# A two-block transformer kernel: the gate table's reads go to GpSimd's queue, and the second token block's search is paced more slowly

## The chip, the cores and the metric

One core of a Trainium2 chip runs the whole program. The metric is device time in microseconds (us), lower is better. A time shown as a median comes from runs without a profile; the trace is of one further, profiled execution.

## What is computed

A sequence of 256 tokens (plus 16 meta tokens), 1024 channels, float32, goes through two blocks. The first block mixes with a state-space scan and then applies PEER, a layer of 16,384 single-neuron experts:

```
q = (t @ w_q).reshape(T, 8, 2, 128)
s = einsum('thsd,hskd->thsk', q, sub_keys)
v_half, i_half = top_k(s, 16)
cand = v_half[:, :, 0, :, None] + v_half[:, :, 1, None, :]
best, pos = top_k(cand, 16)                      # per token and head
experts = i1 * 128 + i2 ;  gates = softmax(best)
act = gelu(einsum('td,tkd->tk', xb, expert_u[experts])) * gates
out = einsum('tk,tkd->td', act, expert_v[experts])
```

The second block is a gated linear recurrence, a convolutional feed-forward layer, windowed attention with sinks and a second feed-forward layer. The change touches only the work around PEER.

## The kernel before

**Dense experts.** The kernel does not gather experts. It multiplies all 256 tokens with all 16,384 rows of `expert_u` (the first expert stage, 128 weight chunks of 128 experts each), applies GELU, multiplies by a gate that is zero where an expert was not chosen, and multiplies the result with all of `expert_v` (the second expert stage, again 128 chunks). The products `hact` stay in on-chip memory between the two stages.

**Weights.** Every weight chunk is a 512 KB tile `raw`, loaded by SyncE (SP) in one queue, in order, into four buffers. ScalarE rounds it to a high part `wh` (three buffers), VectorE subtracts to get a low part `wl` (three buffers), and TensorE makes three products of high and low parts for each chunk. The load of a chunk waits until `wl` of the chunk four before it has been made, since that frees its buffer.

**The gates** of the two blocks of 128 tokens come in two ways. For the first block (`tb` 0), the search (`topk1(0)`, `topk2(0)`) finds the places, and GpSimd scatters 128 columns of values into a table `gtab` in device memory (128 indirect writes, zeroed earlier). In the second expert stage `w_split(j2)` reads a piece `gts` of that table for each pair of chunks (64 reads of 128 KB, `g_load`, two buffers) and VectorE multiplies it into `hact`; ScalarE then makes `wth` (the rounded `hact`) and VectorE `wtl` (its low part), which are TensorE's stationary operands. For the second block (`tb` 1), `topk1(1)` and `topk2(1)` search, a TensorE transpose puts the indices into `idxT`, and `g_side(1)` builds one-hot tiles `oA`, `oB`, multiplies them on TensorE into `sm` and multiplies the gates into `hact`, four tokens a step, during the first expert stage.

**What sets the order.** Main-line code calls `wa` for each chunk of the first expert stage. After each chunk `tick()` advances the side generators by their rates: a generator that yields a cost c at rate r consumes c / r chunks. That is the order in which instructions are emitted; a scheduler then places them on each engine from its own estimates, and every engine runs its list strictly in order. `g_load(j2 + 2)` is emitted in `w_split(j2)`, right after the multiplication that empties the buffer; loads 0 and 1 are emitted three pairs before the end of the first expert stage.

Of the kernel before, what the change touches and what calls it, by code (L numbers as in the profile page):

```python
# [208 lines left out]
def build(tc, a, out):  # L209
    nc = tc.nc  # L210
    top = ExitStack()
    with top:
# [54 lines left out]
        V, S, PE, SP = nc.vector, nc.scalar, nc.tensor, nc.sync  # L267
# [157 lines left out]
        def wait(cond):  # L425
            while not cond():
                yield
# [314 lines left out]
        gtv = gtab.rearrange("(a c) o -> a (c o)", a=128)  # L742
# [282 lines left out]
        def score(tb, c):  # L1025
            return scores[:, tb * 16 + c]
# [19 lines left out]
        def top16(vals, idxs, src, w, part):  # L1046
            if part == 0:
                V.max(out=vals[:, 0:8], in_=src)
                V.max_index(out=idxs[:, 0:8], in_max=vals[:, 0:8], in_values=src)
                V.match_replace(out=w, in_to_replace=vals[:, 0:8], in_values=src, imm_value=-3.0e38)  # L1050
            else:
                V.max(out=vals[:, 8:16], in_=w)
                V.max_index(out=idxs[:, 8:16], in_max=vals[:, 8:16], in_values=w)

        def topk1(tb):
            for c in range(16):
                yield from wait(lambda: c in ust["sc"])
                w = gp.tile([128, 128], F, name="sw", bufs=1)
                for part in range(2):
                    top16(vh[:, c], ih[:, c], score(tb, c), w, part)  # L1060
                    yield 0.4 if part else 0.6
            ust["topk"] = tb
# [77 lines left out]
        def after(ins, others):  # L1140
            for other in others:
                tc.add_manual_dep(ins.ins, other.ins.name, mybir.DependencyInfo(
                    mybir.DependencyClass.Sync, mybir.DependencyReason.DATA), reason="the same places")
# [54 lines left out]
        def paced(gen, rate):  # L1198
            for c in gen:
                yield (1.0 if c is None else c) / rate  # L1200

        def peer_side():
            yield from paced(topk1(0), 1.3)
            yield from paced(topk2(0), 1.3)

            yield from paced(topk1(1), 1.1)
            yield from paced(topk2(1), 1.1)
            yield from paced(g_side(1), 1.25)

        skp = Pool(0, 16, 8)  # L1210
# [17 lines left out]

        add_side(u_norm())
        add_side(peer_side())  # L1230
        for c in range(16):
            qs = sk_load(c)
# [29 lines left out]
        gts = {}  # L1262

        def g_load(j2):
            gts[j2] = gtp.tile([128, 2, 128], F, name="gts")
            ins = SP.dma_start(gts[j2].rearrange("p j t -> p (j t)"), gtv[:, j2 * 256:(j2 + 1) * 256])
            after(ins, last)

            tc.add_manual_dep(ins.ins, st["mm"].ins.name, mybir.DependencyInfo(
                mybir.DependencyClass.NoSync, mybir.DependencyReason.SCHED_ONLY), reason="order")  # L1270

        for j2 in range(64):
            if j2 == 61:
                g_load(0)
                g_load(1)
            if j2 == 46:
                while ust["topk"] < 1:
                    step_sides()
            pp = bank("acc").rearrange("p (j t) -> p j t", j=2)
            for j in range(2):  # L1280
                wa(pp[:, j], xTh, xTl, T0, 256)
            u_post(j2, pp)
# [6 lines left out]
        def w_split(j2):  # L1289
            wth = wp.tile([128, 2, 256], FR, name="wth")  # L1290
            wtl = wp.tile([128, 2, 256], FR, name="wtl")
            g = gts.pop(j2)
            for _, tsl, hv_ in Hact(2 * j2, 2 * j2 + 2, 0, 128):
                tt(hv_, hv_, g, OP.mult)
            if j2 + 2 < 64:
                g_load(j2 + 2)
            for _, tsl, hv_ in Hact(2 * j2, 2 * j2 + 2, 0, 256):
                act(wth[:, :, tsl], hv_, AF.Copy)
                tt(wtl[:, :, tsl], hv_, wth[:, :, tsl].bitcast(F), OP.subtract)
            wts[j2] = (wth, wtl)  # L1300
# [473 lines left out]
```

## Time and profile before

| what | value |
|---|---|
| median of 3 runs | 1685.29 us (1683.22 to 1690.29) |
| the profiled execution's own time | 1680.89 us |
| its span in the trace | 1679.1 us |
| TensorE busy | 1657.2 us |
| VectorE busy | 1219.5 us |
| ScalarE busy | 949.6 us |
| GpSimd busy | 242.6 us |

The profiled execution is the reference for every duration below; it is 4.4 us under the median of the other runs. Matmuls overlap, so that TensorE counts as busy even where its rate drops: the rate is read from how many matmuls start in a stretch, or from the distance between starts.

### The profile page before, as it was taken

Reading aid. Unit: us, or ns where it says so; the run is one execution under the profiler, and the core shown is the slowest. Engines: PE = TensorE matmul, PEld = TensorE weight load, DVE = VectorE, ACT = ScalarE, POOL = GpSimd, SP = SyncE. Lnnn points to the kernel's source line nnn. Section 1 sums busy time; section 2 is a strip of 40 time slices with the busy share of each in tenths; the row PEclk is TensorE's granted clock in tenths of the full one; section 3 lists DMA queues with packets and bytes.
Section 4 is the critical chain, followed back from the end, with each engine's and each line's share of the span. In section 5 each row is a group of like instructions: output and inputs, shape, how many; then the busy total and the mean of one; then the engine's idle time right before and its main releaser. Section 6 shows DMA issues by size and latency. Waiting matters only on the chain. (4 is left out here: it accounts for less than half of the span.)

```text
span 1679.1 us, 29135 instructions
## 1 busy us (share of the span) xinstructions
PE 1657.2 (99%) x11114; PEld 1498.8 (89%) x11114; DVE 1219.5 (73%) x2388; ACT 949.6 (57%) x1590; POOL 242.6 (14%) x132
## 2 busy tenths in 40 slices
PE   8999999999999999999999999999999999999998
PEld 6999889999999999877777788998899988899986
DVE  6789768999567874555555666987787757887754
ACT  6877556544478874444444455733565545765543
POOL 0000000187887870000000000000000000000000
PEclk9999999999999999999999999999999999999999
DMA  8844465577766666666666696634566655346663
GB/s 268 284 133 132 151 204 177 164 173 174 206 172 145 149 154 186 196 210 197 205 204 209 221 325 207 188 114 143 164 192 188 187 175 174 101 162 182 187 186 114
DMA packets 118205, 306.59 MB, mean 183 GB/s; under 512 B 28961, under 2 KB 47905, under 8 KB 117810
## 3 DMA queue, kind: packets, MB, share of 16 engines
q1 hardware_dynamic: 99634, 304.67, 58.4%
q0 software_dynamic: 18432, 0.07, 2.7%
q8 instruction: 87, 1.43, 0.4%
q14 instruction: 52, 0.43, 0.1%
HBM read 294.14 MB, written 10.55 MB: 181 GB/s over the span
## 5 line engine op out<-in xcount | busy, mean ns | idle before, releaser
L290 ACT ACTIVATE wh<-raw 128x1024 fp32r<-128x1024 f32 x523 | 552.3, 1057 | 484.4 <-PE acc L272 426.2
L278 DVE TENSOR_TENSOR wl<-raw,wh 128x1024 fp32r<-128x1024 f32 x523 | 634.3, 1222 | 210.6 <-ACT wh L290 206.0
L272 PE MATMUL acc<-xTh,wh 128*128 128x256 f32 (+2 forms) x2184 | 541.0, 286 | 0.3 <-ACT xTh L290 0.3
L272 PE MATMUL acc<-xTl,wh 128*128 128x256 f32 (+2 forms) x2184 | 533.8, 282 | 1.0 <-DVE xTl L278 1.0
L272 PEld LDWEIGHTS acc<-xTh,wh 128*128 128x128 f32 x2184 | 411.4, 189 | 3.3 <-issue 1.7
L272 PEld LDWEIGHTS acc<-xTl,wh 128*128 128x128 f32 x2184 | 412.3, 189 | 2.2 <-DVE xTl L278 1.2
L272 PE MATMUL acc<-xTh,wl 128*128 128x256 f32 (+2 forms) x2184 | 307.0, 282 | 1.8 <-DVE wl L278 1.6
L1150 POOL DMA_INDIRECT gtab<-gval,gplace x128 | 242.4, 1893 | 389.1 <-DVE gplace L287 328.5
L272 PEld LDWEIGHTS acc<-xTh,wl 128*128 128x128 f32 x2184 | 279.1, 188 | 4.0 <-DVE wl L278 3.9
L272 PE MATMUL acc<-wl,wth 128*128 128x512 f32 x512 | 205.7, 402 | 3.0 <-DVE wl L278 2.8
L272 PE MATMUL acc<-wh,wth 128*128 128x512 f32 x512 | 202.2, 395 | 0.0
L272 PE MATMUL acc<-wh,wtl 128*128 128x512 f32 x512 | 161.5, 394 | 0.0
L272 PEld LDWEIGHTS acc<-wl,wth 128*128 128x128 f32 x512 | 96.4, 188 | 37.6 <-DVE wl L278 16.7
L272 PEld LDWEIGHTS acc<-wh,wtl 128*128 128x128 f32 x512 | 96.4, 188 | 22.4
L272 PEld LDWEIGHTS acc<-wh,wth 128*128 128x128 f32 x512 | 96.4, 188 | 20.9 <-ACT wh L290 0.2
L278 DVE TENSOR_TENSOR hactA<-hactA,gts 128x256 f32<-128x256 f32 x48 | 20.3, 426 | 117.0 <-DMA gts<-gtab 117.0
L272 PE MATMUL acc<-wh,fl 128*128 128x512 f32 x176 | 69.6, 395 | 0.0
L272 PE MATMUL acc<-wl,fh 128*128 128x512 f32 x176 | 69.5, 395 | 0.0
L272 PE MATMUL acc<-wh,fh 128*128 128x512 f32 x176 | 69.5, 395 | 0.0
L290 ACT ACTIVATE wth<-hactA 128x512 fp32r<-128x512 f32 x48 | 30.2, 632 | 60.7 <-PE acc L272 57.0
L272 PE MATMUL acc<-wh,xTh 128*128 128x512 f32 x112 | 47.1, 421 | 0.7 <-ACT wh L290 0.7
L272 PE MATMUL acc<-wl,xTh 128*128 128x512 f32 x112 | 45.0, 403 | 0.5 <-DVE wl L278 0.5
(329 smaller groups left out, 2060.5 us busy)
## 6 DMA issues: line engine op xcount, KB each, us to landing
raw<-in_u SPq DMA_DIRECT2D x128, 512.0 KB, 3.7
raw<-in_v SPq DMA_DIRECT2D x128, 512.0 KB, 4.4
raw<-in_up SPq DMA_DIRECT2D x88, 512.0 KB, 3.6
raw<-in_w_in SPq DMA_DIRECT2D x45, 512.0 KB, 3.7
raw<-in_dn SPq DMA_DIRECT2D x44, 512.0 KB, 3.6
raw<-in_hg_in SPq DMA_DIRECT2D x32, 512.0 KB, 4.1
gtab<-zero SPq DMA_DIRECT2D x16, 512.0 KB, 6.7
raw<-in_w_out SPq DMA_DIRECT2D x16, 512.0 KB, 3.6
```

Source lines behind the costliest of these rows:

```text
L272: st["mm"] = PE.matmul(o, l, r, start=start, stop=stop_)
L278: V.tensor_tensor(out=o, in0=x, in1=y, op=op)
L290: S.activation(o, i, f, **kw)
L1150: ins = nc.gpsimd.indirect_dma_start(out=gtab, out_offset=bass.IndirectOffsetOnAxis(ap=gplace[:, c].bitcast(U32), axis=0), in_=gval[:, h, ...
```

## The change

`peer_side` paces the second block's search at 0.8 in place of 1.1, so that each of its steps takes 1.375 times as many chunks. `g_load` issues its 64 reads from GpSimd (`nc.gpsimd`) and no longer from SyncE; what they wait for is still the scatters and the buffer.

```diff
@@ -1203,8 +1203,8 @@
             yield from paced(topk1(0), 1.3)
             yield from paced(topk2(0), 1.3)
 
-            yield from paced(topk1(1), 1.1)
-            yield from paced(topk2(1), 1.1)
+            yield from paced(topk1(1), 0.8)
+            yield from paced(topk2(1), 0.8)
             yield from paced(g_side(1), 1.25)
 
         skp = Pool(0, 16, 8)
@@ -1263,7 +1263,7 @@
 
         def g_load(j2):
             gts[j2] = gtp.tile([128, 2, 128], F, name="gts")
-            ins = SP.dma_start(gts[j2].rearrange("p j t -> p (j t)"), gtv[:, j2 * 256:(j2 + 1) * 256])
+            ins = nc.gpsimd.dma_start(gts[j2].rearrange("p j t -> p (j t)"), gtv[:, j2 * 256:(j2 + 1) * 256])
             after(ins, last)
 
             tc.add_manual_dep(ins.ins, st["mm"].ins.name, mybir.DependencyInfo(
```

**In the queues.** SyncE's list from the end of the first expert stage into the second: in the rows with a minus, a read of the gate table stands after every two weight loads; with a plus, what is there now.

```order
 L350 DMA raw<-in_u 128x1024 x128
-L1266 DMA gts<-gtab 128x256 x2
-L350 DMA raw<-in_v 128x1024 x6
-L1266 DMA gts<-gtab 128x256
+L350 DMA raw<-in_v 128x1024 x98
+L1323 DMA hold<-hsp 128x2048
+L350 DMA raw<-in_v 128x1024 x2
```

The reads have left the list of weight loads. GpSimd's list holds the scatters of the first block's gates, and now the 64 reads after them, with nothing else in between:

```order
 L1770 UNCONDITIONAL_BRANCH
 L1150 DMA gtab<-gval,gplace 2097152x1 x128
+L1266 DMA gts<-gtab 128x256 x64
 L1770 UNCONDITIONAL_BRANCH
 L1770 ISA
```

**The search on VectorE.** This is the first place at which VectorE's list differs at all; `cdw` and `ih` are the last operations of the second block's search, the copy to `idxT` follows TensorE's transpose, and `oB` begins `g_side(1)`.

```order
 L278 TENSOR_TENSOR cdw<-cdw,ihf 128x512
 L1120 TENSOR_REDUCE ih<-cdw 128x32
-L278 TENSOR_TENSOR wl<-raw,wh 128x1024 x22
+L278 TENSOR_TENSOR wl<-raw,wh 128x1024 x37
 L1136 COPY idxT<-tr 128x384
 L284 TENSOR_SCALAR oB<-cst,idxT 128x128 x8
 L278 TENSOR_TENSOR wl<-raw,wh 128x1024
```

Every row up to the search's last one stands where it stood; `idxT`, and `g_side(1)` after it, come 15 chunks later. On TensorE the last product `sm` of `g_side(1)` stands 24 chunks ahead of the second expert stage before, and 7 chunks now.

**VectorE at the end of the first expert stage, after the change.** The rows run from the last product `sm` of `g_side(1)` to the first multiplications with `gts`, those of pairs 0 and 1.

```order
L278 TENSOR_TENSOR hactA<-sm,hactA 128x4x96
L278 TENSOR_TENSOR hactB_6373<-sm,hactB_6373 128x4x24
L278 TENSOR_TENSOR wl<-raw,wh 128x1024
L278 TENSOR_TENSOR hactB_6373<-acc,hactB_6373 128x256
L278 TENSOR_TENSOR hactA<-hactA,gts 128x2x128 x2
L278 TENSOR_TENSOR wl<-raw,wh 128x1024
L278 TENSOR_TENSOR wtl<-hactA,wth 128x512 x2
```

Before the change the last product `sm` stood far ahead of these rows; now one `wl` lies between it and the first use of `gts`.

## Rows read from the trace of the kernel before

**Rows 1.** The page's head: the span, and busy time of TensorE.

```profile
span 1679.1 us, 29135 instructions
...
PE 1657.2 (99%) x11114; PEld 1498.8 (89%) x11114; DVE 1219.5 (73%) x2388; ACT 949.6 (57%) x1590; POOL 242.6 (14%) x132
```

**Rows 2.** Six stretches: length, busy time (instructions) by engine, granted clock, DMA share, GB/s.

```profile
700.00:740.00 40.00, 40.00 (x173) 32.16 (x172) 23.23 (x29) 19.33 (x23) 0.00 (x0) 1.00 0.63 207
740.00:940.00 200.00, 197.93 (x830) 153.34 (x830) 112.87 (x138) 91.05 (x104) 0.00 (x0) 1.00 0.64 205
1000.00:1040.00 40.00, 40.00 (x173) 32.41 (x173) 24.71 (x36) 20.69 (x29) 0.00 (x0) 1.00 0.69 226
300.00:365.00 65.00, 65.00 (x552) 65.00 (x551) 64.66 (x238) 32.58 (x39) 31.76 (x15) 1.00 0.66 170
365.00:430.00 65.00, 63.19 (x511) 61.02 (x511) 63.20 (x198) 30.45 (x36) 48.68 (x28) 1.00 0.74 176
480.00:630.00 150.00, 150.00 (x1288) 150.00 (x1287) 118.45 (x230) 127.45 (x320) 118.24 (x70) 1.00 0.68 151
```

**Rows 3.** Waits between 740 and 940 us: us in total, times, longest.

```profile
DVE hactA L278 <- DMA gts<-gtab: 85.0, 34, 3.2
...
PEld acc L272 <- DVE wl L278: 12.8, 32, 1.1
```

**Rows 4.** Timeline of the second expert stage: start, length, idle before.

```profile
801.27 0.42 DVE L278 TENSOR_TENSOR hactA<-hactA,gts 128x256 f32<-128x256 f32 x1 [2.31 <-DMA gts<-gtab]
...
801.61 2.35 DVE L278 TENSOR_TENSOR wl<-raw,wh 128x1024 fp32r<-128x1024 f32 x2
...
802.86 0.33 SPq L350 DMA_DIRECT2D raw<-in_v  x1
...
803.24 0.42 SPq L1266 DMA_DIRECT2D gts<-gtab  x1
...
804.16 0.40 PE L272 MATMUL acc<-wh,wth 128*128 128x512 f32 x1
...
807.03 0.43 DVE L278 TENSOR_TENSOR hactA<-hactA,gts 128x256 f32<-128x256 f32 x1 [2.46 <-DMA gts<-gtab]
...
808.34 0.40 PE L272 MATMUL acc<-wh,wth 128*128 128x512 f32 x1
...
808.65 0.19 PEld L272 LDWEIGHTS acc<-wl,wth 128*128 128x128 f32 x1 [0.35 <-DVE wl L278]
```

**Rows 5.** VectorE's timeline: multiplications with `gts` of pairs 5 and 48.

```profile
708.74 0.43 DVE L278 TENSOR_TENSOR hactA<-hactA,gts 128x256 f32<-128x256 f32 x1 [2.39 <-DMA gts<-gtab]
...
957.45 0.42 DVE L278 TENSOR_TENSOR hactB<-hactB,gts 128x256 f32<-128x256 f32 x1 [2.37 <-DMA gts<-gtab]
```

**Rows 6.** The tile `gts`: ns min/median/max, first and last start; landing min/median/max.

```profile
L1266 SPq DMA_DIRECT2D gts<-gtab x64: 326/424/434, 671.2 to 1037.5; - x64
...
DMA to landing us min/median/max: 3.5/3.8/6.4
```

**Rows 7.** The tile `gtab`, in the same columns (its landing row covers all DMAs).

```profile
L1150 POOL DMA_INDIRECT gtab<-gval,gplace x128: 1543/1580/3577, 329.0 to 629.3; - x128
...
DMA to landing us min/median/max: 3.0/3.9/7.8
```

**Rows 8.** Waits between 365 and 430 us.

```profile
PEld acc L272 <- DVE wl L278: 3.9, 10, 0.6
...
PE acc L272 <- DVE wl L278: 1.6, 5, 0.4
```

**Rows 9.** The tile `oB`: TensorE's products of `g_side(1)`.

```profile
L272 PE MATMUL sm<-oB,oA x256: 273/275/275, 484.3 to 620.2; 128*128 128x128 f32 x128
```

**Rows 10.** ScalarE's timeline near 960 us, then TensorE's wait between 940 and 1000.

```profile
959.25 1.28 ACT L290 ACT_TABLE_LOAD   x1 [4.81 <-DVE lbe L278]
...
PE acc L272 <- DVE wl L278: 0.8, 1, 0.8
```

**Rows 11.** The tile `wth`: TensorE's products of the second expert stage.

```profile
L272 PE MATMUL acc<-wh,wth x512: 387/393/479, 688.5 to 1055.7; 128*128 128x512 f32 x171
```

## The prediction

> **What bounds the kernel now.** I read the page first: TensorE is busy for nearly the whole span [rows 1]. That number cannot show a loss of rate, because matmuls overlap, so I went to stretches and counted matmuls. In the second expert stage 40 us hold 173 matmuls of 512 columns where the stage runs well, early in it and late in it; 200 us in the middle hold 830, where 173 per 40 us would make 865 [rows 2]. So about 35 matmuls' time, 35 x 0.231 = 8 us, goes missing there. In the search's part of the first expert stage 65 us hold 511 matmuls of 256 columns, against 552 in the 65 us before them: 41 x 0.118 = 4.8 us missing [rows 2]. These are the two places at which the change is aimed; the granted clock is full in both, so the clock is no part of it [rows 2].
>
> The waits say what is late in the middle of the second expert stage. VectorE sits idle 34 times, 85 us in all, for a read of the gate table, and TensorE's weight loads wait 32 times for `wl`, which VectorE makes after that idle time [rows 3]. The timeline shows why the read is late: it is a loop. A read is issued at 803.24, the multiplication that needs it starts at 807.03, two `wl` follow it as they do at 801.61, and SyncE's next weight load goes out when the first of those is done, as at 802.86; the next read stands behind that load in SyncE's list [rows 4]. The buffer of the read had been free long before. The loop's length is its landing (803.24 to 807.03, 3.8 us, the median of all 64 [rows 6]) plus the path from the multiplication's start to the next issue (801.27 to 803.24, 1.97 us [rows 4]): 5.76 us for a pair of chunks.
>
> TensorE alone needs less. From 804.16 to 808.34 lie 18 matmuls without a stall, 0.2322 us each [rows 4], so a pair of chunks, 24 matmuls, takes 5.573 us. Over 43 pairs the loop took (957.45 - 708.74) / 43 = 5.784 us [rows 5]. It is slower than TensorE by 0.211 us a pair, and at 808.65 TensorE's weight load pays 0.35 us of it [rows 4].
>
> **The change part by part.**
>
> *The reads leave SyncE's queue.* GpSimd issues a read when the buffer is empty, right after the multiplication two pairs earlier; its list holds nothing but these reads after the scatters, and GpSimd is idle in this stage [rows 2]. The read then has two pairs minus one multiplication to land: 2 x 5.573 - 0.43 = 10.7 us. The trace has no plain read issued from GpSimd. From below, it costs what SyncE's cost, 3.5 us [rows 6]; from above, I take the worst of GpSimd's indirect writes, 3.6 us on the engine and a landing of 7.8 us from the issue [rows 7], counted one after the other: 11.4 us. The nearer rows are the medians, 1.6 and 3.9 us [rows 7], since the read also has 128 pieces and GpSimd is not crowded; 5.5 us at most, half the room. So the loop is gone, VectorE's wait for the gates goes, and the next thing to be late is TensorE itself: VectorE works 112.87 us in 34.5 pairs, 3.3 us a pair, and ScalarE 2.6 us [rows 2], both well below 5.573.
>
> The gain: 43 x 0.211 = 9.1 us of loop, less what TensorE's lead still covered. In 700 to 740 us the rate is that of the undisturbed stretch [rows 2], so the 5.5 pairs between 708.74 and 740 cost nothing: 37.5 x 0.211 = 7.9 us. Then one stall of 0.8 us near 963 us: ScalarE waits 4.81 us for a small VectorE operation that stands behind a late gate multiplication, and its weights come late [rows 10]; this goes too. Together 8.7 us. What remains between TensorE's first product of this stage and its last, 688.5 to 1055.7 [rows 11], I leave as it is.
>
> SyncE loses 64 issues of 0.42 us [rows 6], off the path: its weight loads now wait only for `wl`.
>
> *The search is paced more slowly: nothing on VectorE.* The lists show it: up to the search's last operation VectorE's rows are the same. The scheduler had put the search as early as its inputs allowed, and the pacing shifts emission, not that place. So the 4.8 us at 365 to 430 us, where TensorE waits for `wl` behind a full VectorE (63.2 of 65 us) [rows 2, 8], stay. What does move is `g_side(1)`, by 15 chunks of 24 matmuls at 65 / 552 us, 2.83 us each [rows 2]: 42 us, so that its products run from about 527 to 668 us and no longer from 484 to 620 [rows 9]. Its work beside the main line costs TensorE nothing where it stands: 1288 matmuls in 150 us, four in a hundred of them shorter ones, and VectorE at 118 of 150 us [rows 2]. Later it meets more finished chunks, so its VectorE multiplications grow and ScalarE's copies shrink; 21% of VectorE is free for that. I cost it at 0; if that cover were gone, each chunk would pay what VectorE exceeds 2.83 us by.
>
> *The end of the first expert stage.* The reads 0 and 1 reuse the memory of `oB`, so they wait for the last product `sm`, now 7 chunks ahead of the second stage: 688.5 - 7 x 2.83 = 668.7 us. With 5.5 us they land at 674, no later than the 671.2 + 3.8 = 675 us at which the median puts them before [rows 6]; with 11.4 us at 680, which would hold VectorE for some 5 us while its `wl` has about one chunk of lead, a cost of 1 to 2 us once. I take 0.
>
> The sum: 1680.9 - 8.7 = 1672.2 us for a profiled execution. The median of the runs shown is 4.4 us above that execution, and I carry the gain over unchanged: 1685.3 - 8.7 = **1676.6 us**. The loop amplifies landing time (0.1 us more costs 4.3 us over 43 pairs), so the slower runs may lose more in it and gain more; that makes the upside of the gain wider than its downside.
>
> **Rivals.**
>
> *Nothing is gained (about 1685).* The gates are still late because GpSimd's reads take as long as the room they have. For it: scatters took up to 3.6 us on the engine and 7.8 us to land [rows 7]. With L from the end of a multiplication to the landing, the new loop is (L + 0.43) / 2 for a pair; it equals the old 5.78 at L = 11.1 us. Against it: the median sum is half of that.
>
> *Slower: the reads starve on GpSimd.* One mechanism: GpSimd must build each read's pieces, VectorE's work keeps it from that, and L passes 11.1 us. Half a per cent over before needs 8.4 + 8.7 us over 62 pairs, a loop of 5.85 us, so L = 11.27; at L = 12.2 the loop is 6.3 us and the time 1676.6 + 62 x 0.74 = 1722 us. Rows against it: while VectorE was full (64.7 of 65 us) GpSimd still issued a scatter every 2 to 4 us [rows 2, 7], and here VectorE works 3.3 us in 5.6. The Trainium skill has a rule that speaks against the change ("SBUF — State Buffer", sections "SBUF: two separate sides" and "Who interferes with whom"): a DMA issued from GpSimd has its descriptors written over a port pair that VectorE can lock for a whole instruction, and it advises the SP or ACT queue. By that rule a lock would last as long as VectorE's busy stretch, and the read would come up to 3.3 us later, 8.8 us by the medians, still inside the room. The same section says that a tensor_tensor has no such lock on the write side, and nearly all of VectorE's work in this stage is of that form; no run here shows which holds.
>
> *The search improves too (about 1672).* If the pacing took the load off VectorE, the 4.8 us at 365 to 430 us would go: 1676.6 - 4.8 = 1671.8. Against it stands the unchanged list.
>
> **How the numbers follow.** The loop goes and the search stays: 0.70, with its own range 1671 to 1680. Nothing gained: 0.15. The search as well: 0.09. Slower: 0.06. Half a per cent, about what a measurement of this kernel can tell from no change, is 8.4 us, or 1676.9; the likeliest value lies almost on it, and as the slower runs should gain more I put two thirds of the first case below it: faster 0.46 + 0.09 = 0.55, same 0.24 + 0.15 = 0.39, slower 0.06. The range runs from the search case with a larger loop loss, 1669, to a full loss of the gain, 1684; outside it lie the slow case and some of the "nothing" case.
>
> **What would show it.** In the changed trace VectorE's wait for `gts` should be near 0 us where it was 85, pairs should follow at 5.57 to 5.6 us, 200 us of the stage should hold 860 matmuls or more, and the stage should take about 358 to 360 us where it took 367 [rows 11]. TensorE should still lose some 4.8 us behind the search, and `oB` should run until about 668 us. The prediction is wrong if VectorE still waits for `gts` for more than a few us in all, if the first products with `wth` start late, or if the matmul count in the search's stretch recovers.

## The result, and the profile after the change

The changed kernel takes 1671.12 us (median of 4 runs, 1670.82 to 1671.19). The kernel before, run beside it, takes 1687.79 us (4 runs, 1683.22 to 1691.14). The ratio is 0.9912, with a 95% interval of 0.9896 to 0.9929. In later sets of 8 to 17 runs the kernel before had medians of 1683.0 to 1684.8 us, so the gain is best put at 12 to 14 us. Between the two profiled executions it is 1680.89 - 1671.19 = 9.7 us; why the medians lie further apart is explained below.

First the stretches of the changed kernel, with the columns of [rows 2].

```profile
365.00:430.00 65.00, 63.15 (x511) 60.96 (x510) 63.73 (x200) 30.19 (x35) 49.03 (x28) 1.00 0.77 174
700.00:740.00 40.00, 40.00 (x174) 32.44 (x173) 24.98 (x30) 19.50 (x23) 4.20 (x8) 1.00 0.63 208
740.00:940.00 200.00, 200.00 (x863) 162.12 (x862) 124.81 (x144) 94.52 (x108) 18.94 (x36) 1.00 0.67 213
940.00:1000.00 60.00, 60.00 (x260) 48.65 (x259) 38.83 (x60) 32.26 (x45) 5.92 (x11) 1.00 0.87 298
1000.00:1040.00 40.00, 40.00 (x174) 32.43 (x173) 26.05 (x36) 20.80 (x29) 2.15 (x4) 1.00 0.64 205
```

The 200 us from 740 now hold 863 matmuls; they held 830 [rows 2]. The search's stretch from 365 still holds 511, as before. The granted clock is full in all these stretches, as it was.

The waits between 740 and 940 us, in the columns of [rows 3]:

```profile
POOL gts L1266 <- DVE hactA L278: 176.4, 35, 5.0
DVE wl L278 <- ACT wh L290: 63.5, 72, 1.5
ACT wh L290 <- PE acc L272: 60.1, 36, 1.7
```

VectorE's wait for `gts` (85 us) and TensorE's for `wl` (12.8 us) [rows 3] are no longer in the list. What waits now is GpSimd, for a buffer to come free, and ScalarE, for TensorE to give a `wh` buffer back: TensorE sets the pace.

The timeline, in the columns of [rows 4]:

```profile
800.20 0.42 DVE L278 TENSOR_TENSOR hactA<-hactA,gts 128x256 f32<-128x256 f32 x1
...
800.92 0.54 POOL L1266 DMA_DIRECT2D gts<-gtab  x1 [5.05 <-DVE hactA L278]
800.95 0.69 DVE L278 TENSOR_TENSOR wtl<-hactA,wth 128x512 fp32r<-128x512 f32 x1 [0.33 <-ACT wth L290]
801.90 1.23 DVE L278 TENSOR_TENSOR wl<-raw,wh 128x1024 fp32r<-128x1024 f32 x1 [0.26 <-ACT wh L290]
...
805.77 0.42 DVE L278 TENSOR_TENSOR hactA<-hactA,gts 128x256 f32<-128x256 f32 x1
806.49 0.54 POOL L1266 DMA_DIRECT2D gts<-gtab  x1 [5.04 <-DVE hactA L278]
```

The two multiplications stand 5.57 us apart, TensorE's own pace for a pair, and neither has idle time in front of it. The read goes out 0.3 us after the multiplication that empties its buffer. At 807.03 the kernel before paid 2.46 us of idle time in front of the same instruction [rows 4].

The order on VectorE is not quite the old one. A `wtl` follows the multiplication at 800.95, and then the `wl`; before, two `wl` followed the multiplication [rows 4] and the `wtl` of the pair before it stood ahead. The scheduler swapped the two, which the prediction did not speak of, and so it has to be tested.

Three tiles, in the columns of [rows 6]: the reads, TensorE's products of `g_side(1)` and those of the second expert stage.

```profile
L1266 POOL DMA_DIRECT2D gts<-gtab x64: 538/538/605, 669.8 to 1018.8; - x64
...
L272 PE MATMUL sm<-oB,oA x256: 273/275/275, 527.3 to 669.0; 128*128 128x128 f32 x128
...
L272 PE MATMUL acc<-wh,wth x512: 390/393/477, 689.0 to 1046.1; 128*128 128x512 f32 x171
```

The second expert stage takes 357.1 us where it took 367.2 [rows 11]; the forecast was 358 to 360.

### The profile page after: what moved, and what is told of

It reads as the page before. It is cut to its first block, busy times and chain, and to the rows that moved or that the text cites. A ratio compares the mean times of both kernels' runs of the same rounds, so it can differ in the third digit from the quotient of the medians.

```text
span 1669.4 us, 29183 instructions
## 1 busy us (share of the span) xinstructions
PE 1650.4 (99%) x11114; PEld 1502.4 (90%) x11114; DVE 1230.1 (74%) x2393; ACT 949.2 (57%) x1571; POOL 279.6 (17%) x196
## 5 line engine op out<-in xcount | busy, mean ns | idle before, releaser
L272 PE MATMUL acc<-wl,wth 128*128 128x512 f32 x512 | 202.0, 394 | 0.0
L1266 POOL DMA_DIRECT2D gts<-gtab x64 | 34.5, 540 | 346.1 <-DVE hactA L278 239.0
```

Source lines behind the costliest of these rows:

```text
L272: st["mm"] = PE.matmul(o, l, r, start=start, stop=stop_)
L1266: ins = nc.gpsimd.dma_start(gts[j2].rearrange("p j t -> p (j t)"), gtv[:, j2 * 256:(j2 + 1) * 256])
```

## The experiments

The theory: a read stood in SyncE's list behind a weight load that waits for a `wl` made after the gate multiplication, so multiplication, `wl`, load, read and landing formed a loop slower than TensorE. The rivals: the pace of the search gave part of the gain; GpSimd's way of moving the data did; VectorE's new order did.

**One half of the change at a time.** `e1_reads_only` is the changed kernel with the old pace; `e2_pace_only` is the kernel before with the new pace.

```diff
# e1_reads_only, against the kernel after
-            yield from paced(topk1(1), 0.8)
-            yield from paced(topk2(1), 0.8)
+            yield from paced(topk1(1), 1.1)
+            yield from paced(topk2(1), 1.1)
```

```diff
# e2_pace_only, against the kernel before
-            yield from paced(topk1(1), 1.1)
-            yield from paced(topk2(1), 1.1)
+            yield from paced(topk1(1), 0.8)
+            yield from paced(topk2(1), 0.8)
```

> Only the reads are issued from GpSimd; the search keeps its pace of 1.1. Loop theory (the reads stood behind weight loads that wait for wl, and that loop of 5.78 us a pair was slower than TensorE's 5.57): the whole gain, 1670.5 to 1672.5 us, VectorE waits for gts about 0 us between 740 and 940 us, about 863 matmuls there. Rival, the pacing gave part of the gain: 1675 us or more here. The search's loss at 365 to 430 us stays at 4.8 us by both, and oB ends at about 620 us.

> Only the search is paced at 0.8; the reads stay in SyncE's list. Loop theory: the loop is as before, so 1683 to 1690 us with the spread of before, 85 us of VectorE's wait for gts between 740 and 940 us, about 830 matmuls there; the end of g_side(1) moves from 620 to 668 us and costs nothing. Rival, the pacing gave part of the gain: 1675 to 1680 us and more than 840 matmuls in the same stretch. Rival, the later g_side(1) costs something that the reads' gain hid: above 1690 us.

Measured: the reads alone 1670.81 us (5 runs, ratio 0.9923, 0.9905 to 0.994), the pace alone 1685.63 us (12 runs, ratio 1.0005, 0.9991 to 1.0018). The reads give the whole gain, the pace none. With the reads alone the 200 us from 740 hold 863 matmuls, and VectorE has no wait for `gts` there. In the pace-only kernel the waits of 740 to 940 us show the old picture:

```profile
DVE hactA L278 <- DMA gts<-gtab: 86.7, 34, 4.6
...
PEld acc L272 <- DVE wl L278: 13.9, 26, 2.5
```

The same 200 us hold 814 matmuls, fewer than the 830 or so that I expected. Its profiled execution took 1686.28 us, 5.4 us longer than that of before. Its multiplications of pairs 5 and 48 (as [rows 5]) tell where:

```profile
707.94 0.43 DVE L278 TENSOR_TENSOR hactA<-hactA,gts 128x256 f32<-128x256 f32 x1 [1.28 <-DMA gts<-gtab]
...
962.44 0.42 DVE L278 TENSOR_TENSOR hactB<-hactB,gts 128x256 f32<-128x256 f32 x1 [3.22 <-DMA gts<-gtab]
```

That is 254.50 us for 43 pairs, 5.92 us each; before it was 248.71 us [rows 5]. The 5.8 us between the two are about the 5.4 us by which the executions differ: between these two executions it is the loop that varies, and in it the landing. Added up over the 43 pairs, the time from a multiplication to the issue of the next read is 84.6 us in both traces; from that issue to the next multiplication it is 164.1 us before and 169.9 us here. One late read makes 2.1 us of that: it went out at 780.34 and took 5.94 us to the multiplication, where 3.8 us is the median landing [rows 6].

```profile
786.28 0.42 DVE L278 TENSOR_TENSOR hactA<-hactA,gts 128x256 f32<-128x256 f32 x1 [4.60 <-DMA gts<-gtab]
```

TensorE then sat idle for 2.06 us until 787.89, for want of `wl`. Right after that the granted clock was at the lower of its two levels, 1.2 GHz, for 3.4 us, and matmuls started 0.43 us apart instead of 0.23. The stretch, in the columns of [rows 2], shows 0.91; the next 10 us show 0.92.

```profile
780.00:790.00 10.00, 7.95 (x30) 6.12 (x31) 4.97 (x6) 3.50 (x4) 0.00 (x0) 0.91 0.49 151
```

**A read in two halves.** To make the loop longer by one issue, `e3_split_sp` cuts each read in two in SyncE's list; `e4_split_pool` does the same to the changed kernel on GpSimd.

```diff
# e3_split_sp, against the kernel before (e4_split_pool: the same with nc.gpsimd, against the kernel after)
-            ins = SP.dma_start(gts[j2].rearrange("p j t -> p (j t)"), gtv[:, j2 * 256:(j2 + 1) * 256])
-            after(ins, last)
+            for hs_ in (slice(0, 64), slice(64, 128)):
+                ins = SP.dma_start(gts[j2][hs_].rearrange("p j t -> p (j t)"), gtv[hs_, j2 * 256:(j2 + 1) * 256])
+                after(ins, last)
...
```

> As the kernel before, with each read of the gate table cut into two halves of 64 partitions, both issued by SyncE, one after the other. Loop theory: the second half leaves 0.42 us later, so the loop grows from 5.78 to about 6.2 us a pair, 0.63 us above TensorE's 5.57, and holds for nearly all 62 pairs: 15 to 30 us slower than before, about 1700 to 1715 us, and about 800 matmuls between 740 and 940 us; if the halves land faster by 0.3 us than the whole, only about 5 us slower. Rival, the reads were late for another reason (the table's place in device memory, the transfer's bandwidth), and not through the loop of issues: two halves in parallel land as early as the whole or earlier, no slower than before.

> As the kernel after the change, with each read cut into the same two halves, both issued by GpSimd. Loop theory: the read has 10.7 us to land there and needs 4 to 5, so one more issue of 0.54 us costs nothing: 1670 to 1672 us, as the changed kernel, and VectorE's wait for gts stays at 0. Rival, GpSimd is near its limit in this stage (its issue held by VectorE): 5 us or more slower than the changed kernel.

Measured: 1671.55 us for the halves on SyncE (ratio 0.9928, 0.9907 to 0.9948) and 1671.05 us on GpSimd (0.9925, 0.9905 to 0.9945). The second is as the theory had it. The first is not what I expected from it: not a slower kernel but the full gain, with every read still in SyncE's list. SyncE's and VectorE's timeline of that kernel shows why.

```profile
799.91 3.12 SPq L350 DMA_DIRECT2D raw<-in_v  x2
...
801.45 1.23 DVE L278 TENSOR_TENSOR wl<-raw,wh 128x1024 fp32r<-128x1024 f32 x1 [0.26 <-ACT wh L290]
...
802.59 0.42 DVE L278 TENSOR_TENSOR hactA<-hactA,gts 128x256 f32<-128x256 f32 x1
...
803.09 1.09 SPq L1267 DMA_DIRECT2D gts<-gtab  x2
```

The scheduler had placed the multiplication one `wl` later. The `wl` that the load waits for (801.45) is now made ahead of the multiplication (802.59), so the load and the reads behind it no longer wait for the multiplication. The kernel had not lengthened the loop but cut it at another place. Either that, or smaller transfers, gave the gain, so the next four kernels keep whole reads and change the order alone.

**Order against queue.** `f1_pool_old_order` keeps the reads on GpSimd and undoes the swap on VectorE. `f2_sp_mul_later` keeps SyncE's list of before and puts only the multiplication one `wl` later. `f3_sp_one_earlier` puts each read one weight load earlier in SyncE's list. `f4_sp_one_later` puts it one later, with VectorE's order as in `f2_sp_mul_later`. In `f3_sp_one_earlier` the weight loads of a chunk are emitted at the end of its turn and bound behind the last read; in `f4_sp_one_later` the read is emitted a chunk later and bound behind the last load. The added lines bind the scheduler's order only and make no engine wait.

```diff
# f1_pool_old_order, against the kernel after (in w_split)
...
-                tt(hv_, hv_, g, OP.mult)
+                m_ = tt(hv_, hv_, g, OP.mult)
+                if "wtl" in st:
+                    tc.add_manual_dep(m_.ins, st["wtl"].ins.name, mybir.DependencyInfo(
+                    mybir.DependencyClass.NoSync, mybir.DependencyReason.SCHED_ONLY), reason="order")
...
-                tt(wtl[:, :, tsl], hv_, wth[:, :, tsl].bitcast(F), OP.subtract)
+                st["wtl"] = tt(wtl[:, :, tsl], hv_, wth[:, :, tsl].bitcast(F), OP.subtract)
```

```diff
# f2_sp_mul_later, against the kernel before (where a chunk is split, and in w_split)
...
-            tt(l, r, h.bitcast(F), OP.subtract)
+            wl_[i] = tt(l, r, h.bitcast(F), OP.subtract)
...
-                tt(hv_, hv_, g, OP.mult)
+                m_ = tt(hv_, hv_, g, OP.mult)
+                if j2 > 2:
+                    tc.add_manual_dep(m_.ins, wl_[2 * j2 + 203].ins.name, mybir.DependencyInfo(
+                    mybir.DependencyClass.NoSync, mybir.DependencyReason.SCHED_ONLY), reason="order")
```

```diff
# f3_sp_one_earlier, against the kernel before (the loads, g_load, and the loop of the second expert stage)
-                SP.dma_start(t, srcs[st["dma"]])
+                w_ = SP.dma_start(t, srcs[st["dma"]])
...
+                if "rd" in st:
+                    tc.add_manual_dep(w_.ins, st["rd"].ins.name, mybir.DependencyInfo(
+                    mybir.DependencyClass.NoSync, mybir.DependencyReason.SCHED_ONLY), reason="order")
...
-            pump_dma()
+            if "hold" not in st:
+                pump_dma()
...
+            st["rd"] = ins
...
+            st["hold"] = 1
             hl = wnext()
...
             if j % 2 == 0 and j // 2 + 1 < 64:
                 w_split(j // 2 + 1)
+            del st["hold"]
+            pump_dma()
```

```diff
# f4_sp_one_later, against the kernel before
...
+            if j2 > 1:
+                tc.add_manual_dep(ins.ins, st["raw"].ins.name, mybir.DependencyInfo(
+                    mybir.DependencyClass.NoSync, mybir.DependencyReason.SCHED_ONLY), reason="order")
...
-            if j2 + 2 < 64:
-                g_load(j2 + 2)
...
             hl = wnext()
+            if j % 2 and j // 2 + 3 < 64:
+                g_load(j // 2 + 3)
```

> The kernel after the change, with VectorE's order within a pair of chunks put back to that of before: the scheduler had moved the gate multiplication ahead of the previous pair's wtl, and here it stands behind it again. Loop theory (the read's place behind a weight load was the cause): reads on GpSimd wait for nothing but their buffer, so the order within the pair is indifferent: 1670.5 to 1672 us, no wait for gts, about 863 matmuls in 740 to 940 us. Rival, VectorE's new order made the gain: back to 1680 us or more.

> The kernel before, whole reads in SyncE's list at their old places; only VectorE's order is changed: the gate multiplication stands one wl later, so that the wl which frees the buffer of the weight load ahead of the next read is made before the multiplication and no longer after it. Loop theory: the issue of the read then no longer depends on the multiplication before it, the loop is cut without moving a read: 1670.5 to 1672.5 us. Rival, what counts is the way of the transfer (queue, size of the pieces): no gain, 1680 us or more, with VectorE waiting some 80 us for gts between 740 and 940 us.

> The kernel before, whole reads still in SyncE's list, but each one weight load earlier in it. Loop theory: the weight load ahead of the read then waits for a wl of the pair before, and the read has a pair's time more: 1670.5 to 1672.5 us, VectorE's wait for gts near 0. Rival, the reads are late since they share SyncE's queue and its transfers with the weights: no gain, 1680 us or more.

> Reads in SyncE's list, each one weight load later in it than before, and VectorE's order that of the kernel whose multiplication stands one wl later. Loop theory: the read stands again behind a load that waits for the first wl made after the multiplication; the loop is closed again, 3.8 + 2.0 = 5.8 us a pair or more: 1680 to 1700 us, VectorE waits 60 us or more for gts between 740 and 940 us. Rival, the order on VectorE alone decides: 1670.5 to 1672.5 us as with the read at its old place.

Measured:

| kernel | median us (runs) | ratio to before, 95% interval |
|---|---|---|
| `f1_pool_old_order` | 1670.70 (4) | 0.9921, 0.9897 to 0.9944 |
| `f2_sp_mul_later` | 1671.23 (4) | 0.9926, 0.9903 to 0.9949 |
| `f3_sp_one_earlier` | 1671.24 (4) | 0.9924, 0.9901 to 0.9947 |
| `f4_sp_one_later` | 1678.93 (10) | 0.9967, 0.9954 to 0.998 |

The swap on VectorE is indifferent when the reads are on GpSimd. With whole reads in SyncE's list the full gain comes either from moving the multiplication by one place or from moving the read by one place. The second of these is not as clean as it was meant to be: in `f3_sp_one_earlier` the scheduler also changed VectorE's order, to that of the changed kernel, with the `wtl` right behind the multiplication.

```profile
800.10 0.42 DVE L278 TENSOR_TENSOR hactA<-hactA,gts 128x256 f32<-128x256 f32 x1
800.59 0.42 SPq L1271 DMA_DIRECT2D gts<-gtab  x1
800.84 0.69 DVE L278 TENSOR_TENSOR wtl<-hactA,wth 128x512 fp32r<-128x512 f32 x1 [0.33 <-ACT wth L290]
```

So what the read's place does by itself is shown by `f2_sp_mul_later` against `f4_sp_one_later`, which have one and the same order on VectorE. The timeline of `f2_sp_mul_later` has the same picture as that of the halves: `wl` first, then the multiplication, then the read; VectorE waits for `gts` 0.8 us in all between 740 and 940.

```profile
801.50 1.22 DVE L278 TENSOR_TENSOR wl<-raw,wh 128x1024 fp32r<-128x1024 f32 x1 [0.26 <-ACT wh L290]
802.64 0.42 DVE L278 TENSOR_TENSOR hactA<-hactA,gts 128x256 f32<-128x256 f32 x1
...
803.13 0.42 SPq L1267 DMA_DIRECT2D gts<-gtab  x1
```

The read one place later closes the loop again, with VectorE's order as in `f2_sp_mul_later`. The timeline of `f4_sp_one_later`:

```profile
796.76 0.43 DVE L278 TENSOR_TENSOR hactA<-hactA,gts 128x256 f32<-128x256 f32 x1 [2.27 <-DMA gts<-gtab]
797.11 1.22 DVE L278 TENSOR_TENSOR wl<-raw,wh 128x1024 fp32r<-128x1024 f32 x1
...
798.35 0.33 SPq L350 DMA_DIRECT2D raw<-in_v  x1
798.73 0.42 SPq L1267 DMA_DIRECT2D gts<-gtab  x1
...
802.43 0.43 DVE L278 TENSOR_TENSOR hactA<-hactA,gts 128x256 f32<-128x256 f32 x1 [2.31 <-DMA gts<-gtab]
```

From the multiplication to the issue it takes 1.97 us, the same as in the kernel before [rows 4], and 3.70 us more to the next multiplication: 5.67 us for a pair that TensorE could do in 5.57; over the 43 pairs from 5 to 48, late reads included, it is 5.77 us. VectorE's wait for `gts` is back, 81.2 us between 740 and 940, and the stretches show the loss:

```profile
740.00:940.00 200.00, 197.79 (x843) 156.07 (x842) 116.92 (x139) 88.64 (x105) 0.00 (x0) 1.00 0.64 205
940.00:1000.00 60.00, 60.00 (x257) 47.76 (x256) 39.98 (x59) 30.95 (x43) 0.00 (x0) 1.00 0.86 294
1000.00:1040.00 40.00, 38.22 (x163) 29.86 (x162) 22.83 (x34) 17.16 (x28) 0.00 (x0) 1.00 0.66 205
```

Against the changed kernel 20 + 3 + 11 = 34 matmuls are missing, 34 x 0.232 = 7.9 us; the two profiled executions differ by 9.1 us, the medians by 7.8 us. Its median lies 1.1 us under the range that I gave for it, so the loop came out a little shorter there than I took it.

**Another list without weight loads.** `g1_reads_act` issues the reads from ScalarE.

```diff
# g1_reads_act, against the kernel before
-            ins = SP.dma_start(gts[j2].rearrange("p j t -> p (j t)"), gtv[:, j2 * 256:(j2 + 1) * 256])
+            ins = S.dma_start(gts[j2].rearrange("p j t -> p (j t)"), gtv[:, j2 * 256:(j2 + 1) * 256])
```

> The kernel before, with the reads of the gate table issued by ScalarE and not by SyncE (nor by GpSimd). Loop theory: any list without weight loads in it cuts the loop: 1670.5 to 1672.5 us, VectorE's wait for gts near 0, about 863 matmuls in 740 to 940 us. Rival, something particular to GpSimd's reads (their larger pieces of 4 KB) made the gain: 1680 us or more.

Measured: 1671.03 us (4 runs, ratio 0.9924, 0.9907 to 0.9942). Nothing particular to GpSimd is needed.

```profile
740.00:940.00 200.00, 200.00 (x863) 162.14 (x862) 124.67 (x143) 94.88 (x108) 0.00 (x0) 1.00 0.67 212
```

**The search, really spread.** In `g2_search_held` each VectorE operation of the second block's search is bound, in the scheduler's order alone, to come after the matmul emitted last, so that the pace decides where the search stands; `g3_search_held_11` does so at the old pace. Both keep the reads on GpSimd.

```diff
# g2_search_held, against the kernel after (g3_search_held_11: 1.1 in place of 0.8); True switches the hold on
...
+                def g(*a_, **k_):
+                    ins = f(*a_, **k_)
+                    tc.add_manual_dep(ins.ins, st["mm"].ins.name, mybir.DependencyInfo(
+                        mybir.DependencyClass.NoSync, mybir.DependencyReason.SCHED_ONLY), reason="order")
+                    return ins
...
-            yield from paced(topk1(1), 0.8)
-            yield from paced(topk2(1), 0.8)
+            yield from paced(topk1(1), 0.8, True)
+            yield from paced(topk2(1), 0.8, True)
```

> The kernel after the change, pace 0.8, with each VectorE operation of the second block's search held, in the scheduler's order alone, behind the matmul emitted last, so that the pace really sets where the search stands on VectorE. If the 4.8 us at 365 to 430 us are lost to a search that is packed too densely, they go or shrink: 1666 to 1668.5 us. Rival, a spread search stands in front of weight parts that are due and costs as much as before or more: 1671 us or above.

> As the held search, at the pace of before, 1.1, still with reads on GpSimd. If only the packing counts, the pace of 1.1 spreads less than 0.8 and keeps part of the 4.8 us: between the held search at 0.8 and the changed kernel, 1667 to 1671 us. Rival, spreading costs more than it gives: nearer to the changed kernel than the held search at 0.8 is, or above it.

Measured: 1666.33 us (5 runs, ratio 0.9898, 0.9884 to 0.9913) and 1666.26 us (4 runs, 0.9896, 0.9879 to 0.9913). They beat the changed kernel by 4.8 and 4.9 us, the size of the loss counted at 365 to 430 us. The stretch of the held search at 0.8:

```profile
365.00:430.00 65.00, 65.00 (x552) 65.00 (x551) 51.29 (x176) 30.18 (x35) 52.69 (x22) 1.00 0.75 187
```

and of the one at 1.1:

```profile
365.00:430.00 65.00, 65.00 (x552) 65.00 (x551) 58.80 (x236) 33.08 (x38) 50.90 (x24) 1.00 0.76 180
```

Either way VectorE is no longer full (51.3 or 58.8 of 65 us, before 63.2 [rows 2]) and all 552 matmuls fit. My expectation that the old pace would keep part of the loss was wrong: what the search lacked was a hold on the scheduler, and with it 1.1 is slow enough.

## Why the prediction was right, and where its size was off

The changed kernel was forecast at 1676.6 us, 1669 to 1684, faster as the likeliest; it is faster, at 1671.1. The time alone would not have told which mechanism was at work: it lies nearer to the rival in which the search improves too (1671.8) than to the forecast. The matmul counts of the two stretches tell them apart. By the prediction's own steps:

- *The reads leave SyncE's queue; the loop is gone.* Right, and shown from both sides: four ways of opening the loop (GpSimd, ScalarE, the read one place earlier, the multiplication one place later) each give 1670.8 to 1671.3 us, and the read one place later closes it. Who issues the reads does not matter. The 3.8 us that the prediction calls the median of all 64 reads is that of the 36 whose landing the trace has; from the issue to the multiplication, which all have, the median of pairs 6 to 48 is 3.78 us, so the loop's length stands.
- *What the read costs on GpSimd.* I took 5.5 us by the medians, out of 10.7 us of room. The trace of the changed kernel has no landing times for these reads; that of `f1_pool_old_order`, which also reads from GpSimd, has them for 24 of the 64, with 3.8 us as median and 5.8 us at worst, issue included:

```profile
DMA to landing us min/median/max: 2.3/3.8/5.8
```

  So the rivals in which GpSimd is too slow, needing 11.1 us and more, were far off. The 64 issues took 538 to 605 ns, and the one at 800.92 ran while VectorE did a `wtl` at 800.95, so no lock shows. The rule that I weighed from the Trainium skill ("SBUF — State Buffer", section "Who interferes with whom") would hold GpSimd's issue for as long as VectorE has the shared port pair. For a tensor_tensor the same section of the Trainium skill infers that the writing of descriptors is not held up; the trace agrees, and as nearly all of VectorE's work there is of that form, this case can't say what happens with others.
- *The search is paced more slowly: nothing on VectorE.* Right: 511 matmuls before and after, and the pace alone gives a ratio of 1.0005. The 4.8 us were real, and the held search takes them.
- *`g_side(1)` moves by 42 us, at no cost.* Forecast 527 to 668 us, measured 527.3 to 669.0. The second expert stage starts at 689.0 and not at 688.5 [rows 11], and the reads-only kernel is 0.3 us faster than the full change, with overlapping runs; a cost, if there is one, is below half a microsecond.
- *The end of the first expert stage.* Read 0 goes out at 669.8, as forecast within a microsecond or so, and VectorE never waits for it.
- *The sum, 8.7 us.* A little small: 9.7 us between the two executions, 10.1 us in the second expert stage. One more stretch of the kernel before, in the columns of [rows 2], completes the count:

```profile
940.00:1000.00 60.00, 59.21 (x251) 46.60 (x250) 39.43 (x59) 30.18 (x43) 0.00 (x0) 1.00 0.84 288
```

  Against the changed kernel 1 matmul came back at 700 to 740 us, 33 at 740 to 940 and 9 at 940 to 1000: 43 x 0.232 = 10.0 us (each count can be off by one). At 700 to 740 that is 0.2 us of the 1.2 us that I had credited to TensorE's lead; at 740 to 940 it is 7.7 us, where 34.5 pairs x 0.211 make 7.3; from 940 on it is 2.1 us, where my terms (three pairs of the loop, and the stall of [rows 10]) make 1.4. Each term was a little short, none was wrong.
- *"I carry the gain over unchanged" from the profiled execution to the median.* This step failed, and it is most of the error: 4.4 of the 5.5 us. I added to the changed kernel the 4.4 us by which the other runs of before lay above its profiled one. But the pace-only kernel shows, for one pair of executions, that such a difference is made in the loop (5.8 us there against 5.4 us in the time), so it goes away with the loop. The spread bears it out: the eight loop-free kernels without a held search lie between 1670.2 and 1672.1 us in all 33 runs, while the kernels with the loop range over 1679 to 1691 us and, for `f4_sp_one_later`, 1674.7 to 1680.3 us. The sum against the profiled execution, 1672.2 us, was the number to forecast. I had noted that the loop amplifies the landing time and used it only for the width of the range.

What stays open: why the landing time differs between executions of one kernel.

## What to carry to other kernels

A list that is worked off in order ties a transfer to whatever the instruction ahead of it waits for. Where an engine waits for a small read again and again, follow the issue and not only the transfer: if the issue stands behind something that the same engine makes after that read, it is a loop, and its length against the bottleneck's pace is what counts. It opens by one place in a list as well as by another queue. And where a stall is such a loop, the spread between executions may sit in it too, so that the time without the loop is to be worked out from the profiled execution itself; the gain against the median is then larger than the gain against that execution.

A pacing rate in the emission order says nothing about an engine's order when a scheduler may pull the work forward: look in the list, and bind the work to the main line if it is to be spread.

## What was not expected of the hardware

The time of the looped kernel varied by 12 us between executions (1679.4 to 1691.0 us in 17 runs) and with the loop open by under 2 us (33 runs of eight kernels). And a read of 128 KB issued from GpSimd moved in fewer pieces than its 128 partitions suggest. The DMA view of the changed kernel from 800 to 812 us, with two reads in it:

```profile
q0 software_dynamic: 96, 0.26, 5.5%
```

That is 96 packets for 0.26 MB, 48 for a read: in the trace, 32 of 4096 bytes and 16 of 4 bytes. In the trace of the kernel before, a read from SyncE's queue moves as 128 packets of 1024 bytes; the prediction had taken 128 pieces for GpSimd's reads as well. The issue of a read holds GpSimd for 0.54 us, where SyncE's takes 0.42 us [rows 6].
